# Hybrid S5 and gMLP encoder layer on one core: the setup transposes of b and c emitted by turns, each group at a tick of its own

## The chip, the core and the metric

The kernel runs on one core of a Trainium2 chip. The metric is the time of one execution in device microseconds (us). The engines of the core are named as the profile names them: PE (TensorE: matmuls, and transposes written as matmuls), PEld (its weight loads), DVE (VectorE), ACT (ScalarE), POOL (GpSimd) and SP (SyncE, which here only issues DMAs). Each engine runs its own list of instructions in order, and instructions of different engines wait for each other by semaphores.

## The reference

One encoder layer, batch 1, 512 positions, model width 1024, all in float32. An RMS norm of x goes through one wide projection w_in, whose columns feed two mixers and two gates. What the change touches is the S5 mixer:

```python
def s5_scan(u, lam_re, lam_im, log_step, b_re, b_im, c_re, c_im, reverse):
    lam = lax.complex(lam_re, lam_im)
    step = jnp.exp(log_step)[:, None]
    lam_bar = jnp.exp(lam * step)
    b_bar = ((lam_bar - 1.0) / lam)[..., None] * lax.complex(b_re, b_im)
    bu = jnp.einsum('gpc,lbgc->lbgp', b_bar, u.astype(jnp.complex64))
    _, states = lax.associative_scan(_linear_recurrence, (a, bu), axis=0, reverse=reverse)
    return jnp.einsum('gcp,lbgp->lbgc', lax.complex(c_re, c_im), states).real
...
    y = jax.nn.gelu(y.transpose(1, 0, 2, 3).reshape(bsz, seq, S5_WIDTH))
    y = y * jax.nn.sigmoid(y @ w_glu.astype(f32))
```

There y holds the D skip, the forward scan and the backward scan. There are 32 groups of 16 channels, each with 64 complex states, in two directions. The second mixer is a gMLP spatial gate (layer norm, a 128 x 128 mixing matrix for each head). The outputs of both are projected (w_proj_a, w_proj_b), gated per channel and added; after that come a cross-attention to 256 memory tokens and a SwiGLU feed-forward layer.

## The kernel before

**Matmuls.** Every large product of float32 operands is three products of rounded halves: an operand is split into hi and lo, hi by a copy on ScalarE (`split`, L85), lo by a subtraction on VectorE (L86). The products hi*hi, lo*hi and hi*lo are summed in PSUM (`mm3`, L358; `product`, L1110). Weights are loaded in blocks of 512 KB into `wraw` (L137, L224), split into `whi` and `wlo`, and used once. A plan lists all blocks in the order of use; `next_w` keeps three loads and two splits ahead of the block in use. PSUM has five banks for the main products and three for the others.

**Stages.** The stages are: norm of x and transposes of it into xn; the w_in products (pt and pf tiles); the w_proj_b products of the gMLP half, which are done with fewer and larger sums of blocks (tiles bx, bq and qv at L1110, with the operands s12 and s4 made by L85 and L86 and a `seed` copy into each qv bank at L1123); then the merge stage, where S5's output enters: four loads ygt (L1222) bring it back from DRAM, they are split into yg_hi and yg_lo, and the w_glu product (L358, pf<-yg_hi) gives the GLU. After that w_proj_a, the output projection, the attention and the feed-forward layer.

**The S5 side program.** S5 is not a stage of its own. `s5_program` is a Python generator: setup, kernels, inputs, scan and outputs yield between small pieces, and these pieces are put between the matmuls of the main stages. After each weight block the main program calls `tick(us)` (L453). A tick adds credit in proportion to the block's matmul time and then runs the generator until the credit is used up; a piece that yields a number costs that much credit, and one that yields None ends the side program's turn until the next tick. Further steps are put off by `later(n, ...)`, n ticks long. The pieces are:

- `s5_setup` (L620): loads of the steps and of lam, b and c; transposes of b and c through PSUM (tile pbc) with copies on ScalarE into raw_b and raw_c; then the powers of lam.
- `s5_kernels`: the tables e, pk, ks and tt of the 16-position blocks (L790 to L846).
- `s5_inputs`: wt by transposes (pw, L864), the products pz (L871), copies into zh (L876, L877).
- `s5_scan` (L893): 62 steps of four operations on VectorE (L898 to L901).
- `s5_outputs`: copies ss of the states (L916, L917), products py (L922 to L924), a gelu y (L929), and stores of y to the DRAM tile yd (L932), for four groups of eight.

`finish_side` runs what is left of it right before the merge stage.

**The order of the instructions.** The Python order is not yet the order on the engines: the framework's scheduler (`schedule_with_timeline_sim=True`) reorders the instructions by a timeline that it estimates, and keeps only those of `keep_in_program_order` as they are written. Among these are the late gain loads g_mem and g_x (`gain`, L471) and the first matmuls. So a step that is emitted some ticks later can change the order of everything that is scheduled after it, on every engine and in SP's list of DMAs.

Of the kernel before, what the change touches and what calls it, by code (L numbers as in the profile page):

```python
# [9 lines left out]
F32 = mybir.dt.float32  # L10
# [7 lines left out]
P = 128  # L18
# [8 lines left out]
G = 32  # L27
C = 16
# [24 lines left out]
def hybrid_layer_kernel(  # L53
# [8 lines left out]
    nc = tc.nc  # L62
# [14 lines left out]
    def bank(name):  # L77
        return pm.tile([P, 512], F32, tag="mm", name=name)

    def aux(name, shape=(P, 512)):  # L80
        return pa.tile(list(shape), F32, tag="aux", name=name)
# [394 lines left out]
    ident = cp.tile([P, P], F32, name="ident")  # L476
# [72 lines left out]
    s5p = s5.enter_context(tc.tile_pool(name="s5", bufs=1))  # L549
# [70 lines left out]
    def s5_setup():  # L620
        A_ = nc.scalar
# [3 lines left out]
        def small():  # L625
            used[0] += 1
            return slab[:, used[0] - 1, :]
# [6 lines left out]
        for i, src in enumerate((s5_lam_re, s5_lam_im)):  # L634
            nc.sync.dma_start(lrows[:, i], src[0].rearrange("d g p -> g d p"))
            ps = aux("plam", (P, G))
# [11 lines left out]
        crow = s5p.tile([P, 2, C // 4, 2, 64], F32, tag="tt", name="crow")  # L648
# [2 lines left out]
                nc.sync.dma_start(crow[:, i, :, d, :], src[0, d].rearrange("g (a b) p -> (g a) b p", a=4))  # L651
        bb = s5p.tile([P, 2, G, C], F32, name="raw_b")
        rows = brow.rearrange("g d p c -> g (d p) c")
        for n in range(2):
            ps = aux("pbc", (P, C // 2, 2 * G))
            for k in range(C // 2):
                nc.tensor.transpose(ps[:, k, :], rows[:, :, 8 * n + k], ident[:2 * G, :2 * G])
            A_.copy(bb.rearrange("p i g c -> p c (i g)")[:, 8 * n:8 * n + 8, :], ps)
            yield None
        cc = s5p.tile([P, 2, G, C], F32, name="raw_c")  # L660
        for i in range(2):
            ps = aux("pbc", (P, C // 4, P))
            for k in range(C // 4):
                nc.tensor.transpose(ps[:, k, :], crow[:, i, k].rearrange("q d p -> q (d p)"), ident)
            A_.copy(cc[:, i].rearrange("p g (a b) -> p b (g a)", a=4), ps)
            yield 0.1
        br, bi, cr, ci = bb[:, 0], bb[:, 1], cc[:, 0], cc[:, 1]
        st["c"] = (cr, ci)

# [1 line left out]
        stp, a, rho, th, n, sn, hs, cs = (small() for _ in range(8))  # L671
# [265 lines left out]
    def s5_program():  # L937
        yield from s5_setup()
        yield from s5_kernels(0)
        yield from s5_kernels(1)  # L940
        while "u" not in st:
            yield None
        zh = s5p.tile([P, NCH, 2, G], F32, name="zh")
        st["zh"] = zh
        for o in range(NO):
            yield from s5_inputs(o)
        while st.get("nz", 0) < 2 * NO:
            yield None
        yield None
        yield from s5_scan()  # L950
        for _ in range(2):
            yield None
        for o in range(NO):
            yield from s5_outputs(o)
            if o + 2 < NO:
                yield from s5_kernels(o + 2)
# [103 lines left out]
    for h in range(H):  # L1060
        ps = bank("psv")
# [56 lines left out]
    def unit_bank(name):  # L1118
        return bank(name).rearrange("p (j t) -> p j t", j=2)
# [45 lines left out]
    for q, ts in ((5, T1), (6, T0)):  # L1165
        for i in range(2):
            k = slice(2 * i, 2 * i + 2)
# [319 lines left out]
    for t0 in (0, 2):  # L1487
        ps = {t: bank(f"pt{t - t0}") for t in (t0, t0 + 1)}
# [77 lines left out]
    ps = [bank("pf0"), bank("pf1")]  # L1566
# [67 lines left out]
    for i, u in enumerate(UNITS):  # L1634
        final = i == len(UNITS) - 1
        x, v = begun
        q = unit_bank("pq")
# [132 lines left out]
    for i in range(2):  # L1770
        p = aux("pcut", (P, 256))
# [37 lines left out]
```

## Time and profile before

| what | value |
|---|---|
| median of 3 runs | 892.44 us (892.33 to 893.95) |
| profiled execution | 893.12 us, span 891.3 us, 1.8 us outside the span |
| granted clock, mean | 0.997 |
| PE busy | 881.1 us, 99% of the span |
| DVE busy | 642.5 us, 72% |
| ACT busy | 487.4 us, 55% |
| moved by DMA | 165.36 MB, mean 186 GB/s |
| scan on DVE | 154.10 to 244.53 us |
| first w_glu matmul | 326.10 us |

Times in the rows of the profile count from the start of the span. A row of the timeline has the start, the duration, the engine, the line of the kernel, the operation, the tiles (out<-in), the shapes and the count; in brackets stands how long the engine sat idle before it and what released it. A row of waits has the waiting engine, tile and line, what it waited for, the total, the count and the longest. A row of windows has, for PE, PEld, DVE, ACT and POOL in this order, the busy time and the count, then the granted clock of PE, the DMA share and GB/s. Successive matmuls overlap in the rows: the time that one costs is the distance from start to start, which is less than its duration. SPq is SP's DMA queue.

### The profile page before, as it was taken

How to read it: one execution, taken by the hardware profiler on the slowest of the kernel's cores; microseconds unless marked ns; L12 is line 12 of the kernel's file. 1: busy time of each engine (PE TensorE's matmuls, PEld its weight loads, DVE VectorE, ACT ScalarE, POOL GpSimd, SP SyncE). 2: the span in 40 equal slices, each digit the busy share in tenths (PEclk: the TensorE clock that was granted, in tenths of full speed). 3: DMA queues.
4: the chain of work that ended last, by engine and by line, in shares of the span. 5: the costliest groups of instructions: out<-in, count | busy, mean ns of one | idle time of the engine just before them, and what ended most of it. 6: DMA issues, size and time to landing. Idle time of an engine off the chain costs nothing.

```text
span 891.3 us, 14796 instructions
## 1 busy us (share of the span) xinstructions
PE 881.1 (99%) x5744; PEld 788.0 (88%) x5744; DVE 642.5 (72%) x1048; ACT 487.4 (55%) x714; POOL 106.9 (12%) x165
## 2 busy tenths in 40 slices
PE   9999999999999999999999999999999999999996
PEld 6788888888889998889899978999999999988875
DVE  5697653889847368658856836676878777899875
ACT  5743994244396254347656534645555455655664
POOL 1005301111032111001001001101121111000010
PEclk9999999999999999999999999999999999999998
DMA  8667456978533789834579747627899999356672
GB/s 255 196 189 182 114 155 177 189 191 190 159 87 84 212 285 268 288 117 140 168 221 256 194 103 197 166 81 181 213 237 233 216 225 249 95 167 207 204 230 102
DMA packets 118408, 165.36 MB, mean 186 GB/s; under 512 B 11825, under 2 KB 84161, under 8 KB 118210
## 3 DMA queue, kind: packets, MB, share of 16 engines
q1 hardware_dynamic: 97474, 135.74, 47.9%
q0 software_dynamic: 20576, 28.15, 19.9%
q8 instruction: 45, 0.74, 0.3%
q10 hardware_dynamic: 288, 0.52, 0.2%
q14 instruction: 25, 0.20, 0.1%
HBM read 157.61 MB, written 46.63 MB: 229 GB/s over the span
## 4 chain that ended last, share of the span: by engine, by line
PE 97%; DMA 1%; SPq 1%; ACT 0%; DVE 0%; issue 0%; POOLq 0%; ACTq 0%
PE pf L358 26%; PE pt L358 17%; PE px L1110 12%; PE dx L358 6%; PE pq L1110 6%; PE dq L358 3%; PE pv L1110 3%; PE bx L1110 3%; PE qx L1110 2%; PE dv L358 2%; PE pz L871 2%; PE pk L814 2%; PE bq L1110 1%; PE qv L1110 1%; PE psc L358 1%; PE qq L1110 1%
## 5 line engine op out<-in xcount | busy, mean ns | idle before, releaser
L86 DVE TENSOR_TENSOR wlo<-wraw,whi 128x1024 fp32r<-128x1024 f32 (+1 forms) x145 | 172.2, 1189 | 101.2 <-ACT whi L85 101.0
L85 ACT CAST whi<-wraw 128x1024 fp32r<-128x1024 f32 (+1 forms) x145 | 148.6, 1026 | 152.2 <-PE pf L358 44.0
L358 PE MATMUL pf<-xn,whi 128*128 128x512 f32 x448 | 139.6, 391 | 0.0
L358 PEld LDWEIGHTS pf<-xn,whi 128*128 128x128 f32 x448 | 83.7, 188 | 17.0
L358 PE MATMUL pf<-xn,wlo 128*128 128x512 f32 x224 | 87.3, 390 | 0.0
L1110 PE MATMUL px<-fn,whi 128*128 128x256 f32 x480 | 83.4, 277 | 0.0
L1110 PEld LDWEIGHTS px<-fn,whi 128*128 128x128 f32 x480 | 72.7, 188 | 0.2
L85 ACT CAST whi<-b 128x1024 fp32r<-128x1024 f32 x40 | 42.2, 1055 | 50.4 <-PE px L1110 27.4
L86 DVE TENSOR_TENSOR wlo<-b,whi 128x1024 fp32r<-128x1024 f32 x40 | 48.9, 1223 | 27.0 <-ACT whi L85 27.0
L1110 PE MATMUL px<-fn,wlo 128*128 128x256 f32 x240 | 66.4, 277 | 0.0
L1110 PE MATMUL pq<-s,whi 128*128 128x256 f32 x320 | 55.0, 276 | 0.0
L358 PE MATMUL dx<-whi,s 128*128 128x512 f32 x170 | 53.4, 390 | 0.4 <-DVE h L1734 0.4
L85 ACT CAST whi<-t 128x1024 fp32r<-128x1024 f32 x30 | 31.6, 1054 | 35.6 <-PE pv L1110 12.4
L86 DVE TENSOR_TENSOR wlo<-t,whi 128x1024 fp32r<-128x1024 f32 x30 | 36.7, 1225 | 19.7 <-ACT whi L85 19.7
L358 PEld LDWEIGHTS pf<-xn,wlo 128*128 128x128 f32 x224 | 42.1, 188 | 8.7
L1110 PEld LDWEIGHTS pq<-s,whi 128*128 128x128 f32 x320 | 48.3, 188 | 0.0
L1110 PEld LDWEIGHTS px<-fn,wlo 128*128 128x128 f32 x240 | 45.1, 188 | 0.0
L358 PE MATMUL pt<-whi,xn 128*128 128x512 f32 x128 | 43.7, 412 | 0.7 <-ACT xn L85 0.7
L1110 PE MATMUL pq<-s,wlo 128*128 128x256 f32 x160 | 44.2, 276 | 0.0
L358 PEld LDWEIGHTS dx<-whi,s 128*128 128x128 f32 x170 | 31.8, 188 | 7.5 <-issue 0.8
L358 PE MATMUL dx<-wlo,s 128*128 128x512 f32 x85 | 33.0, 390 | 0.0
L275 POOL DMA_DIRECT2D dsum<-in_w_down_dram x12 | 13.3, 1105 | 162.4 <-DMA dsum<-in_w_down_dram 162.4
(453 smaller groups left out, 2296.8 us busy)
## 6 DMA issues: line engine op xcount, KB each, us to landing
wraw<-in_w_in_dram SPq DMA_DIRECT2D x36, 512.0 KB, 4.7
dsum<-in_w_down_dram SPq DMA_DIRECT2D x20, 512.0 KB, 5.4
wraw<-dsum SPq DMA_DIRECT2D x20, 512.0 KB, 4.1
b<-in_w_gate_dram SPq DMA_DIRECT2D x15, 512.0 KB, 5.4
b<-in_w_up_dram SPq DMA_DIRECT2D x15, 512.0 KB, 5.3
wraw<-in_w_down_dram SPq DMA_DIRECT2D x15, 512.0 KB, 4.4
dsum<-in_w_down_dram POOLq DMA_DIRECT2D x10, 512.0 KB, 8.1
dsum<-dsum POOLq DMA_DIRECT2D x10, 512.0 KB, 8.5
```

Of the source, the lines that this page charges most:

```text
L85: hi = nc.scalar.copy(dst_hi, src)
L86: lo = nc.vector.tensor_tensor(dst_lo, src, dst_hi.bitcast(F32), ALU.subtract)
L275: plan[j + step][1].append((0, lambda d=dst, x=more: nc.gpsimd.dma_start(d, x, accum_op=ALU.add)))
L358: m = nc.tensor.matmul(ps, a[x], b[y], start=start and i == 0, stop=stop and i == 2, skip_group_check=free)
L814: nc.tensor.matmul(ps[32 * j:32 * j + 32, q, :], bd[i][:, g].rearrange("p d c -> p (d c)"), lc(es[i], g), start=(i == 0), stop=False, tile ...
L871: nc.tensor.matmul(ps[:, g, :], wt[:, g, :], u[:, o * GO + g, :], start=True, stop=True)
L1110: nc.tensor.matmul(ps[:, j, :], a[x], b[y], start=start and j == k == i == 0, stop=k == 3 and i == 2, skip_group_check=True)
```

## The change

In `s5_setup`, the transposes of b and c used to come as b, b, c, c, with a None after each b group and 0.1 us of credit after each c group. Now a None stands after the loads, ahead of the first transposes, and the groups come as b, c, b, c with a None after each. The transposes, copies and loads are the same, and the tile raw_c is allocated earlier.

```diff
         rows = brow.rearrange("g d p c -> g (d p) c")
+        cc = s5p.tile([P, 2, G, C], F32, name="raw_c")
+        yield None
         for n in range(2):
             ps = aux("pbc", (P, C // 2, 2 * G))
             for k in range(C // 2):
                 nc.tensor.transpose(ps[:, k, :], rows[:, :, 8 * n + k], ident[:2 * G, :2 * G])
             A_.copy(bb.rearrange("p i g c -> p c (i g)")[:, 8 * n:8 * n + 8, :], ps)
             yield None
-        cc = s5p.tile([P, 2, G, C], F32, name="raw_c")
-        for i in range(2):
             ps = aux("pbc", (P, C // 4, P))
             for k in range(C // 4):
-                nc.tensor.transpose(ps[:, k, :], crow[:, i, k].rearrange("q d p -> q (d p)"), ident)
-            A_.copy(cc[:, i].rearrange("p g (a b) -> p b (g a)", a=4), ps)
-            yield 0.1
+                nc.tensor.transpose(ps[:, k, :], crow[:, n, k].rearrange("q d p -> q (d p)"), ident)
+            A_.copy(cc[:, n].rearrange("p g (a b) -> p b (g a)", a=4), ps)
+            yield None
         br, bi, cr, ci = bb[:, 0], bb[:, 1], cc[:, 0], cc[:, 1]
```

## The prediction

> **What bounds the kernel now.** I read the page first (span, busy shares, the chain that ended last), then TensorE's waits.
>
> ```profile
> span 891.3 us, 14796 instructions
> PE 881.1 (99%) x5744; PEld 788.0 (88%) x5744; DVE 642.5 (72%) x1048; ACT 487.4 (55%) x714; POOL 106.9 (12%) x165
> ...
> PE 97%; DMA 1%; SPq 1%; ACT 0%; DVE 0%; issue 0%; POOLq 0%; ACTq 0%
> ```
>
> ```profile
> PE idle L556 <- DVE mhalf L481: 1.1, 1, 1.1
> PE pt L358 <- ACT ot_hi L85: 0.9, 2, 0.7
> PE pt L358 <- ACT xn L85: 0.7, 1, 0.7
> PE dx L358 <- DVE h L1734: 0.4, 1, 0.4
> ```
>
> TensorE is busy 99% of the span, it carries 97% of the chain, and its waits come to 1.1 + 0.9 + 0.7 + 0.4 = 3.1 us in all. The kernel is TensorE's list of matmuls with nothing between them. The first wait stands ahead of all code in question. So a change of order can win at most about 2 us here, and it loses whatever hole it opens in that list. The question is only: which instruction of TensorE finds its operand late in the new order?
>
> **The transposes themselves.** The change keeps all of them: 16 of b and 8 of c, and four copies out of PSUM on ScalarE.
>
> ```profile
> 30.93 1.09 PE L657 MATMUL pbc<-ident,brow 64*128 64x64 f32 x8
> ...
> 35.99 0.60 PE L664 MATMUL pbc<-ident,crow 128*128 128x128 f32 x4
> ```
>
> Per group they take 1.09 and 0.60 us, before and after: nothing added, nothing removed, 0 us in the sum. What the edit changes is when the S5 side program gets past them. A bare yield ends the side program's turn until the next tick. There were two such yields (after the b groups) and two that cost 0.1 us of credit; now there are five, the new first one ahead of any transpose. So the rest of the S5 chain (parameters, powers, input products, scan) is emitted about three ticks later, and the planner builds another order out of it on all engines. Comparing the two orders of instructions, engine by engine, I find the following.
>
> **The scan starts 6.6 us later.** The scan on VectorE waits for the last pz products and their copies.
>
> ```profile
> 149.99 1.89 PE L871 MATMUL pz<-u,wt 128*128 128x64 f32 x16
> ```
>
> ```profile
> 154.10 0.22 DVE L898 TENSOR_TENSOR sa<-zh,ca 128x64 f32<-128x64 f32 x1 [2.16 <-ACT zh L877]
> ...
> 244.30 0.23 DVE L901 TENSOR_TENSOR zh<-sa,sb 128x64 f32<-128x64 f32 x1
> ```
>
> Ahead of the last pz, TensorE's list now holds 29 more pf matmuls of 512 columns (272 where there were 243). A matmul of that size takes 0.23 us from start to start: in the rows below two of them lie between 13.19 and 13.65.
>
> ```profile
> 11.51 0.63 PE L358 MATMUL pt<-wlo,xn 128*128 128x512 f32 x1
> 11.94 0.98 PE L358 MATMUL pt<-whi,xn 128*128 128x512 f32 x2
> ...
> 13.19 0.62 PE L358 MATMUL pt<-whi,xn 128*128 128x512 f32 x2
> 13.65 0.40 PE L358 MATMUL pt<-wlo,xn 128*128 128x512 f32 x1
> ```
>
> 29 x 0.227 = 6.6 us. The scan's own length does not change (244.53 - 154.10 = 90.4 us), so it ends at about 244.5 + 6.6 = 251.1. TensorE had other work throughout the scan before, and its list is full there after too; this delay alone costs nothing. It matters by what stands behind it.
>
> **First hole: qv after the scan.** The first qv product of the merged w_proj_b part started at 277.11. Behind the scan, ScalarE's rows before are:
>
> ```profile
> 244.56 1.10 ACT L916 COPY ss<-zh 64x504 f32<-64x504 f32 x1 [0.88 <-DVE zh L901]
> ...
> 253.37 1.05 ACT L85 CAST whi<-wraw 128x1024 fp32r<-128x1024 f32 x1
> ...
> 255.87 1.28 ACT L929 ACT_TABLE_LOAD   x1
> 257.16 0.60 ACT L929 ACTIVATE y<-py 128x512 f32<-128x512 f32 x1
> 257.65 1.11 ACT L916 COPY ss<-zh 64x504 f32<-64x504 f32 x1
> ...
> 264.11 2.18 ACT L85 CAST s<-zf 128x512 fp32r<-128x512 f32 x4
> ...
> 268.57 0.58 ACT L1123 COPY qv<-bx 128x512 f32<-128x512 f32 x1
> ```
>
> ```profile
> 255.25 0.39 PE L923 MATMUL py<-ss,e 128*128 128x64 f32 x2
> ...
> 255.92 0.39 PE L923 MATMUL py<-ss,e 128*128 128x64 f32 x2
> ...
> 265.52 0.49 PE L814 MATMUL pk<-e,bd 128*32 128x128 f32 x3
> ...
> 265.99 0.49 PE L814 MATMUL pk<-e,bd 128*32 128x128 f32 x3
> ...
> 277.11 0.28 PE L1110 MATMUL qv<-yb_hi,whi 128*128 128x256 f32 x1
> ...
> 278.05 0.28 PE L1110 MATMUL qv<-yb_hi,wlo 128*128 128x256 f32 x1
> ```
>
> Before, the copy that fills the qv bank was done at 269.15, 8 us ahead of its use. After, TensorE gets there earlier: 24 py matmuls and 15 pairs of pk pieces that stood ahead now stand behind. Three py take 255.92 - 255.25 = 0.67, so 24 are 5.3 us; two pairs of pk take 0.47, so 15 are 3.5 us. Demand: 277.1 - 5.3 - 3.5 = 268.3. ScalarE's list from the scan's end to that copy is now: eight ss copies (244.56 to 253.37, 8.8), part 0.5 (as y, which is as large), four s copies 2.2, part 0.5, one whi 1.0, table load 1.3, y 0.5, four more ss copies 4.5, two s copies 1.1, one whi 1.0, qv 0.6: 22.0 us, so it is ready at 273.1. TensorE waits 273.1 - 268.3 = 4.8, with one pk piece in the middle, whose e operand VectorE rebuilds late. A weight cast that now stands at the scan's end may hold the chain up by 1 us more. I take 5.0; bounds 0 (if the scan starts as before, or ScalarE gets ahead) and 7.
>
> **Second hole: the next qv.** After the second group of py, ScalarE's order is four ss copies, a whi cast, the copy for qv; the copies are released by the last py, as in
>
> ```profile
> 275.25 1.13 ACT L916 COPY ss<-zh 64x504 f32<-64x504 f32 x1 [1.33 <-PE py L924]
> ```
>
> 4 x 1.13 + 1.05 + 0.58 = 6.2 us. TensorE has 34 matmuls of 256 columns and one pk to run meanwhile; eight take 278.05 - 277.11 = 0.94, so 34 are 4.0, and 4.2 with the pk. It waits 2.0 us; bounds 0 and 3.
>
> **Third and largest hole: the GLU's input.** The last S5 outputs go through DRAM (yd) and come back as four ygt loads; a cast of each feeds the first GLU matmul.
>
> ```profile
> 318.44 1.77 SPq L1222 DMA_DIRECT2D ygt<-yd  x4
> ...
> 331.33 0.53 SPq L471 DMA_DIRECT2D g_x<-in_xattn_norm_g_dram  x1
> ```
>
> ```profile
> 330.19 0.68 DVE L1173 TENSOR_TENSOR part<-zf,part 128x512 f32<-128x512 f32 x1
> ```
>
> ```profile
> 326.10 0.63 PE L358 MATMUL pf<-yg_hi,whi 128*128 128x512 f32 x2
> ```
>
> ```profile
> 330.00:336.00 6.00, 6.00 (x28) 4.99 (x27) 3.35 (x5) 3.37 (x6) 1.20 (x1) 1.00 1.06 385
> ```
>
> ```profile
> wraw<-in_w_proj_a_dram SPq DMA_DIRECT2D x4, 512.0 KB, 8.4
> ...
> ygt<-yd SPq DMA_DIRECT2D x4, 256.0 KB, 4.1
> ...
> yd<-y SPq DMA_DIRECT2D x4, 32.0 KB, 2.3
> ```
>
> Before, the ygt loads were issued at 318.44, behind only the two w_glu loads, 7.7 us ahead of the GLU at 326.10, which then did not wait. In the new order of SP's queue they stand behind w_proj_a, qsum, w_proj_a, g_mem and g_x. g_x waits for the L1173 that closes the part tile, as the rows show (330.19 + 0.68, then 331.33), and that L1173 waits for the last bq matmul, the one directly ahead of the GLU on TensorE. So the ygt loads can only be issued after TensorE has run dry. Call that moment G. Two operations of 0.68 (L1132, L1173) with their starts end at G + 1.6; g_x takes 0.53; the first ygt is issued at G + 2.2. Best landing: the 4.1 us of before, then a cast of 0.55: G + 6.9. Worst landing: the 8.4 us that loads took in the crowd: G + 11.2. For the middle I count bytes: five loads of 512 KB, the first two from about G - 3; at 385 GB/s some 1.4 MB are through by G + 2.2, 1.2 MB and the first 0.26 MB remain, 3.8 us, or up to 6.1 us with the 2.3 us that even a small yd store needs. With the cast: G + 6.6 to G + 8.9. I take 7.8; bounds 6 and 11. The three other ygt land 0.7 us apart and the next stage's operands are made behind the late GLU: another 0.8, bounds 0 and 2.
>
> **The clock.** At the end of the span the granted clock falls after TensorE has stopped:
>
> ```profile
> 884.20:884.70 0.50, 0.24 (x3) 0.04 (x1) 0.24 (x2) 0.23 (x2) 0.50 (x1) 1.00 0.00 0
> ...
> 886.50:886.80 0.30, 0.00 (x0) 0.00 (x0) 0.00 (x0) 0.00 (x0) 0.30 (x1) 0.50 0.00 0
> ```
>
> The last matmul ends at 884.44 (0.24 us into the first row); 2 us later the clock is 0.50. And at the start the matmuls of the first dense 3 us run at half the rate (11.51 to 11.94: 0.43 for one) until about 12.7. So the first and the third hole, both longer than 2 us, should each be followed by about 3 us at half rate, in which 1.5 us of work is lost: 3.0 us for two; bounds 0 and 4.
>
> [...]
>
> **Sum.** 5.0 + 2.0 + 7.8 + 0.8 + 3.0 = 18.6 us on the profiled execution's 893.1 (span 891.3 and 1.8 around it): 911.7. The median of the runs shown is 0.7 lower, so I predict 911.
>
> **Rivals.**
> (a) Only the GLU hole opens. If ScalarE reaches the qv copies 5 us sooner than I count, or the scan loses less than 2 us, the first two holes close: 7.8 + 0.8 + 1.5 = 10.1, about 902.5. For it: the first hole is a difference of two long sums. Against it: the scan's shift is a plain count of matmuls.
> (b) All holes open and the ygt loads meet the full crowd: hole 11, tail 2, the clock lower for 4 us after each: 5 + 2 + 11 + 2 + 4 = 24, about 916.5. For it: 1.06 of DMA share around 330. Against it: the crowd before consisted of loads that are now behind ygt.
> (c) No difference: every late operand is covered. That needs the ygt loads issued at least 7 us ahead of G, against their place behind g_x. 892.4.
> (d) Faster: the later S5 chain lets ScalarE deliver the xn and ot_hi casts in time, and no hole opens. The two waits are 1.6 us together, so 890.8. It decides only if the ygt loads are issued before G - 7, and the two waits lie in stages whose order hardly changes.
>
> **Chances.** The forecast with its own range 907 to 915: 0.55; (a) 0.22; (b) 0.14; (c) 0.03; (d) 0.06. A difference below 0.2% (1.8 us) can't be told from none here. Faster 0.06, same 0.03, slower 0.91. The range takes in (a) and (b) and 1.5 us below and above them, for the bounds of their own holes: 901 to 918.
>
> **What would show it.** Right: in TensorE's waits a pf L358 <- yg_hi (or ygt) line of 6 to 11 us, and qv L1110 <- ACT qv L1123 lines of 3 to 7 us together; ygt issued after g_x, later than the last bq matmul; last L901 near 251; half clock in the windows after the holes; after 345 us everything shifted by the same 18 us. Wrong: ygt ahead of g_x, the last L901 at 245, or 0.2 us matmuls directly behind a hole of 8 us (then 3 us less).

## The result, and the profile after

The changed kernel takes 917.3 us (median of five runs, 915.4 to 919.4) against 892.7 (892.3 to 894.0): ratio 1.0273, 95% interval 1.0255 to 1.0291, so 24.6 us slower. The forecast was 911, range 901 to 918. The profiled execution is the slowest of the five: 919.42, span 917.7, 26.4 us over the span before.

The page of the changed kernel (span, busy shares), and TensorE's waits:

```profile
span 917.7 us, 14794 instructions
...
PE 887.4 (97%) x5744; PEld 792.5 (86%) x5744; DVE 643.6 (70%) x1048; ACT 485.2 (53%) x712; POOL 106.8 (12%) x165
```

```profile
PE pf L358 <- ACT yg_hi L85: 9.4, 1, 9.4
PE pk L814 <- DVE e L795: 4.4, 1, 4.4
PE qv L1110 <- ACT qv L1123: 3.3, 2, 1.8
PE pt L358 <- ACT xn L85: 2.3, 1, 2.3
```

The three holes are there, at the three tiles named: 9.4 us ahead of the GLU, 4.4 for one pk piece and 1.5 more for the first qv, 1.8 for the second qv; 17.1 us in all, where the kernel before had none of them. The timeline shows the GLU hole's cause in the rows of VectorE, SP's queue, ScalarE and TensorE:

```profile
341.15 0.69 DVE L1173 TENSOR_TENSOR part<-zf,part 128x512 f32<-128x512 f32 x1
```

```profile
341.87 0.35 SPq L471 DMA_DIRECT2D g_x<-in_xattn_norm_g_dram  x1
342.64 1.96 SPq L1222 DMA_DIRECT2D ygt<-yd  x4
```

```profile
349.14 0.62 ACT L85 CAST yg_hi<-ygt 128x512 fp32r<-128x512 f32 x1 [7.79 <-DMA ygt<-yd]
```

```profile
340.11 0.28 PE L1110 MATMUL bq<-s,wlo 128*128 128x256 f32 x1
349.81 0.79 PE L358 MATMUL pf<-yg_hi,whi 128*128 128x512 f32 x1 [9.43 <-ACT yg_hi L85]
```

TensorE's last bq matmul ends at 340.39; only then can the last L1173 run (by way of L1132, which reads bq), behind it g_x, and behind that, 2.25 us after TensorE went dry, the first ygt load. Its cast starts 6.5 us after that issue and takes 0.6: together the 9.4 us of the hole.

Most of what is left of the loss is the clock. In windows (PE, PEld, DVE, ACT, POOL busy with counts, then the granted clock, DMA share, GB/s):

```profile
277.40:281.40 4.00, 3.95 (x18) 3.95 (x19) 3.04 (x3) 0.97 (x1) 0.00 (x0) 0.50 0.40 131
281.50:285.50 4.00, 4.00 (x37) 4.00 (x37) 3.13 (x4) 1.36 (x2) 0.00 (x0) 1.00 0.40 130
...
302.00:305.30 3.30, 3.30 (x16) 3.30 (x17) 3.30 (x4) 1.76 (x3) 2.10 (x4) 0.50 0.50 70
...
343.00:349.80 6.80, 0.00 (x0) 0.00 (x0) 0.01 (x1) 0.62 (x1) 1.34 (x2) 0.50 1.02 311
349.80:353.10 3.30, 3.29 (x8) 2.61 (x9) 1.87 (x3) 1.24 (x2) 0.00 (x0) 0.50 1.14 279
353.20:357.00 3.80, 3.80 (x18) 3.11 (x18) 0.79 (x2) 1.90 (x2) 0.00 (x0) 1.00 1.09 392
```

Behind each hole, the second one too, matmuls ran at half clock: 18 of them instead of 37 in four us behind the first. The stretches of work at half clock are 4.0, 3.4 and 3.3 us, so 2.0 + 1.7 + 1.7 = 5.4 us were lost there.

One part of the profiled run does not come from the change. In its first 24 us the order is that of before, but a row that stood at 18.19 before (`pt<-whi,xn`, three matmuls) stands at

```profile
18.86 0.80 PE L358 MATMUL pt<-whi,xn 128*128 128x512 f32 x1 [2.31 <-ACT xn L85]
...
21.59 1.07 PE L358 MATMUL pt<-whi,xn 128*128 128x512 f32 x3
```

3.4 us later, behind a wait of 2.31 us for xn (ScalarE sat 1.74 us behind a late load of the S5 steps) and a stretch at half clock, from 18.64 to 22.05. Other kernels below have the same order there and start without it, or have it with no edit there.

The account of the profiled run: start 3.4, holes 17.1, half clock 5.4, waits inside and behind the GLU 1.0 (its stage, from the start of the first yg_hi matmul to the start of the last ya matmul, took 32.46 us before and 35.10 after; 1.7 of the 2.64 us more are the clock): 26.9 against a span that grew by 26.4.

### The profile page after: what moved, and what is told of

It is laid out like the page before. It is cut to its first block, busy times and chain, and to the rows that moved or that the text cites. A ratio compares the mean times of both kernels' runs of the same rounds, so it can differ in the third digit from the quotient of the medians.

```text
span 917.7 us, 14794 instructions
## 1 busy us (share of the span) xinstructions
PE 887.4 (97%) x5744; PEld 792.5 (86%) x5744; DVE 643.6 (70%) x1048; ACT 485.2 (53%) x712; POOL 106.8 (12%) x165
## 4 chain that ended last, share of the span: by engine, by line
PE 67%; ACT 1%; DMA 1%; issue 1%; DVE 1%; SPq 0%; POOLq 0%; ACTq 0%; DVEq 0%
PE pt L358 12%; PE px L1110 12%; PE pf L358 9%; PE dx L358 6%; PE pq L1110 6%; PE dq L358 3%; PE pv L1110 3%; PE qx L1110 2%; PE bx L1110 2%; PE dv L358 2%; PE qv L1110 2%; PE psc L358 1%; PE qq L1110 1%; PE po L358 1%; PE ptr L520 1%; PE bq L1110 1%
## 5 line engine op out<-in xcount | busy, mean ns | idle before, releaser
L358 PEld LDWEIGHTS pt<-whi,xn 128*128 128x128 f32 x128 | 24.9, 197 | 9.4 <-ACT xn L85 2.9
```

The source lines that it names most:

```text
L358: m = nc.tensor.matmul(ps, a[x], b[y], start=start and i == 0, stop=stop and i == 2, skip_group_check=free)
```

## Experiments

**1. Which part of the edit costs: the tick or the turns?** One kernel takes only the new yield, in the order b, b, c, c; one takes only the turns, with the old number of ticks.

```diff
-        rows = brow.rearrange("g d p c -> g (d p) c")
+        rows = brow.rearrange("g d p c -> g (d p) c"); yield None
         for n in range(2):
```

> The kernel before (groups b, b, c, c with their old yields) with one edit: the bare yield ahead of the first transposes. Theory (what costs is that the S5 side program falls a tick behind; the turns of b and c cost nothing): the same holes as in the changed kernel, TensorE waits of 9 to 10 us at the GLU for yg_hi, 5 to 6.5 us for the pk and the first qv, 1.5 to 2 us at the second qv, last L901 about 10 us later than in the kernel before in a run whose start is equal 6 us, and a time of 915 to 920. Rival (the emission by turns costs, through the order of the copies on ScalarE): 892 to 894, no such wait.

Measured: 916.9 us (916.1 to 917.0; ratio 1.0254, 1.0225 to 1.0283). TensorE's waits:

```profile
PE pf L358 <- ACT yg_hi L85: 9.2, 1, 9.2
PE pk L814 <- DVE e L795: 4.4, 1, 4.4
PE qv L1110 <- ACT qv L1123: 3.3, 2, 1.8
```

The bare yield alone gives all holes to 0.2 us. Its profiled run has no late start: span 915.3, scan from 160.64 to 250.77, its start 6.5 us later than before.

The turns alone are the changed kernel with these lines put back:

```diff
         cc = s5p.tile([P, 2, G, C], F32, name="raw_c")
-        yield None
...
             A_.copy(cc[:, n].rearrange("p g (a b) -> p b (g a)", a=4), ps)
-            yield None
+            yield 0.1
```

> The changed kernel without its bare yield ahead of the first transposes and with the old 0.1 after each c group: b, c, b, c by turns, but as many ticks as before. Theory (the ticks): 892 to 894, scan starts at 154, ygt loads ahead of g_x, no wait at the GLU. Rival (the turns): 910 or more, with the holes of the changed kernel.

Measured: 893.95 us against 894.42 for the kernel before on the same chip, ratio 0.9998 (0.9983 to 1.0013). No difference. The scan starts at 154.37, and SP's queue has the order of before from start to end:

```profile
318.59 1.77 SPq L1222 DMA_DIRECT2D ygt<-yd  x4
...
327.41 0.51 SPq L471 DMA_DIRECT2D g_mem<-in_mem_norm_g_dram  x1
...
331.47 0.53 SPq L471 DMA_DIRECT2D g_x<-in_xattn_norm_g_dram  x1
```

So emitting b and c by turns costs nothing, and the tick costs everything.

**2. Does it grow with the ticks?** Two more kernels add ticks in other places: one only replaces 0.1 by None after the c groups of the kernel before, the other has None after each of four groups by turns, without the first one.

```diff
-            yield 0.1
+            yield None
         br, bi, cr, ci = bb[:, 0], bb[:, 1], cc[:, 0], cc[:, 1]
```

> The kernel before with one edit: a bare yield after each c group instead of 0.1 of credit; order b, b, c, c. Theory (any tick more in the setup moves the scan behind the same later pz): the holes of the changed kernel, 915 to 918. Rival (only the tick ahead of the first transposes matters, since it delays the b copies): 892 to 896.

Measured: 918.9 us (a single run), waits for yg_hi 9.1, pk 4.4, qv 3.3. Its first 24 us hold the same late start as the changed kernel's profile (a 2.3 us wait for xn).

```diff
         cc = s5p.tile([P, 2, G, C], F32, name="raw_c")
-        yield None
         for n in range(2):
```

> The changed kernel without the yield ahead of the first transposes, but with a bare yield after each of the four groups. Theory (any tick more in the setup moves the scan by the same step): the holes of the changed kernel, 915 to 918. Rival (the loss grows with the number of ticks): less than the changed kernel, 900 to 912.

Measured: 917.9 us (a single run), waits 9.2, 4.4, 3.3. The kernel before and the turns alone have two bare yields; one has three, two have four, the changed kernel five. All beyond two show the same holes. The loss is a step, not a slope, and the b copies are not needed for it. The traces show why a step: from 172 us on (the scan has begun by then) the lists of instructions of all five engines are the same, place by place, in the four kernels with more than two bare yields. The planner comes to one and the same order from any of them; why it does was not tried.

**3. The GLU hole alone.** In the kernel before, g_mem and g_x are emitted ahead of the ygt loads, and those are kept behind them on SP. The S5 chain is as early as before.

```diff
+    g_mem, g_x = gain(mem_norm_g, "g_mem", True), gain(xattn_norm_g[0], "g_x", True)
     for m in range(4):
-        nc.sync.dma_start(ygt[:, m, :], yd[m].rearrange("p l n -> p (l n)"))
+        in_order(nc.sync.dma_start(ygt[:, m, :], yd[m].rearrange("p l n -> p (l n)")))
```

> The kernel before with g_mem and g_x emitted ahead of the four ygt loads, and these kept in that order on SP: the GLU hole alone, with the S5 chain as early as before. Theory: a wait for yg_hi of 9 to 11 us, half clock for 5 to 10 us around it, and nothing else: 903 to 906. Rival (the early S5 chain leaves slack that hides the loads' place): 892 to 896.

Measured: 908.2 us (907.3 to 909.0) against 894.4, ratio 1.0158 (1.0129 to 1.0187). The only new wait:

```profile
PE pf L358 <- ACT yg_hi L85: 11.7, 1, 11.7
```

The scan ends at 244.66 as before, the GLU starts at 338.04 instead of 326.10, and the clock is at half from 330.71 to 340.95, 2.9 us of it over work. The place of four loads in a queue, alone, costs 14 us; the span grew by 14.6: 11.7 of hole, 1.5 of clock, and 1.4 of which 1.1 lie behind the last ya matmul and were not followed up. The 906 I gave as the upper end is 2.2 us too low: the hole is longer than the 11 allowed, and longer than in the changed kernel. The first ygt load is issued 1.9 us after the last bq matmul here, so no later than there, but it takes 8.8 us to land (328.26 to 337.04).

**4. What holds the ygt loads in the changed kernel?** Here g_mem and g_x are queued behind the last ygt load.

```diff
-        nc.sync.dma_start(ygt[:, m, :], yd[m].rearrange("p l n -> p (l n)"))
+        ld = nc.sync.dma_start(ygt[:, m, :], yd[m].rearrange("p l n -> p (l n)"))
...
-    g_mem, g_x = gain(mem_norm_g, "g_mem", True), gain(xattn_norm_g[0], "g_x", True)
+    with tc.issue_after(ld.ins): g_mem, g_x = gain(mem_norm_g, "g_mem", True), gain(xattn_norm_g[0], "g_x", True)
```

> The changed kernel with g_mem and g_x queued on SP behind the last ygt load; the rest of the order stays. Theory (the GLU hole is made by the place of the ygt loads behind g_x, which waits for the last bq products): the ygt loads are issued about 2.5 us sooner against the last bq matmul, the hole falls from 9.4 to about 7, the time by 2 to 3 us, to 914 to 916. What is left of the hole then belongs to the later yd stores and the loads of w_proj_a and qsum ahead. Rival (g_x is not what holds them, the DMA traffic is): hole and time unchanged, 9 to 10 us and 916 to 919.

Measured: 912.7 us (911.5 to 913.1), ratio 1.0207 (1.0178 to 1.0236). The waits, and SP's rows:

```profile
PE pf L358 <- ACT yg_hi L85: 6.9, 1, 6.9
PE pk L814 <- DVE e L795: 4.4, 1, 4.4
PE qv L1110 <- ACT qv L1123: 3.3, 2, 1.9
```

```profile
335.36 3.19 SPq L1222 DMA_DIRECT2D ygt<-yd  x4
338.59 0.43 SPq L471 DMA_DIRECT2D g_mem<-in_mem_norm_g_dram  x1
339.12 0.37 SPq L471 DMA_DIRECT2D g_x<-in_xattn_norm_g_dram  x1
```

The first ygt load goes out 0.3 us after the last bq matmul (which ends at 335.04) instead of 2.25 us, and the hole falls by 2.5 us. 6.9 us remain without g_x. The w_proj_a and qsum loads stay ahead, and the last y is stored closer to the GLU: in the changed kernel its stores are issued from 334.56, 5.8 us ahead of G, where before it was 312.19, 13.9 us ahead of 326.10. How these two share the rest was not taken apart.

The time fell by 4.6 us between the medians, more than the 2 to 3 expected. The profile has no half clock behind the second hole, which this edit does not touch; by the account above that is worth 1.7 us (the last section shows where that hole lay in time).

**5. The holes behind the scan.** First, pins of order, meant to put the third group's ss copies behind the qv copy on ScalarE, and the s12 subtractions behind the rebuilding of e on VectorE. Pinned are one of the group's four copies and the casts and subtractions of s12.

```diff
-            nc.scalar.copy(s[lo_, :, 1:NCH], zv[lo_, :, 0:NCH - 1])
+            (in_order if o == 2 and i == 0 else (lambda q: q))(nc.scalar.copy(s[lo_, :, 1:NCH], zv[lo_, :, 0:NCH - 1]))
...
-            split(bops[q][0][:, k], bops[q][1][:, k], zf[i][:, :, ts])
+            pinned[0] = True; split(bops[q][0][:, k], bops[q][1][:, k], zf[i][:, :, ts]); pinned[0] = False
```

> The changed kernel with two pins of order after the scan: the third group's ss copies on ScalarE behind the qv copy, and the s12 subtractions on VectorE behind the rebuilding of e; the scan ends as late. Theory (the first hole is made by what stands ahead of the qv copy and of e in these two lists, 4.5 us of ss copies among it): no wait of pk for e, the first qv wait 3.5 to 5 us instead of 4.4 + 1.5, the second below 1.5, and 913 to 915.5. Rival (the late end of the scan alone makes the hole, whatever stands behind it): both waits as in the changed kernel, 916 to 918.

Measured: 915.0 us (913.4 to 915.4), ratio 1.0241 (1.0216 to 1.0265).

```profile
PE pf L358 <- ACT yg_hi L85: 9.6, 1, 9.6
PE qv L1110 <- ACT qv L1123: 5.7, 2, 4.4
```

The waits are as expected, but the pins did less than was meant. ScalarE's rows:

```profile
266.68 1.07 ACT L917 COPY ss<-zh 64x504 f32<-64x504 f32 x1
...
270.86 0.58 ACT L1123 COPY qv<-bx 128x512 f32<-128x512 f32 x1
...
273.36 1.10 ACT L916 COPY ss<-zh 64x504 f32<-64x504 f32 x1
```

Only the pinned copy, and two casts of s, now stand behind the qv copy; the group's other three copies are still ahead of it. On VectorE e comes no sooner: it is ready 21.0 us behind the scan's end, against 20.6 in the changed kernel. The wait for e is gone because the pk pair that waited stands behind the first qv products in TensorE's new list (at 276.78). So this run does not show that the order on VectorE made the wait. What moved is the qv copy: it is done 20.7 us behind the scan's end instead of 22.7, and the two qv waits are 4.4 and 1.3 us instead of 4.4 + 1.5 and 1.8. That is 2.0 us less, with the scan ending just as late. The time's interval overlaps that of the changed kernel; it is the rows that carry this.

Second, half of the ss copies go to GpSimd.

```diff
-            nc.scalar.copy(s[hi_, :, 0:NCH - 1], zv[hi_, :, 0:NCH - 1][:, :, ::-1])
+            nc.gpsimd.tensor_copy(s[hi_, :, 0:NCH - 1], zv[hi_, :, 0:NCH - 1][:, :, ::-1])
```

> The changed kernel with one of each two ss copies (L917) on GpSimd instead of ScalarE: ScalarE's list between the end of the scan and the qv copies is 4 to 6 copies of 1.1 us shorter. Theory (ScalarE's list makes the holes after the scan): pk and the second qv do not wait any more, the first qv waits 0 to 3 us, GLU hole as before at 9 to 11 us, 909 to 913. Rival (GpSimd is much slower at such a copy than ScalarE, so py comes late instead): new waits of py for ss, 915 or more.

Measured: 914.2 us (911.9 to 914.7), ratio 1.0231 (1.0208 to 1.0253); the expected 909 to 913 was missed. TensorE's waits:

```profile
PE pf L358 <- ACT yg_hi L85: 14.1, 1, 14.1
PE qv L1110 <- ACT qv L1123: 2.0, 1, 2.0
```

GpSimd does such a copy in 1.0 to 2.1 us, and no wait of py for ss appears. The holes behind the scan shrink from 7.7 to 2.0 us. ScalarE's list is confirmed as what made the qv waits: TensorE's last bq matmul ahead of the first hole ends 16.2 to 16.3 us behind the scan's end in the changed kernel, with the pins and here alike, while the first qv copy is done after 22.7, 20.7 and 18.2 us, and the hole follows it (e is sooner here as well, 16.3 us behind the scan: VectorE rebuilds it behind subtractions that sit idle for ScalarE's s casts, 8.7 us in the changed kernel; and the pk pair stands behind the first qv products again).

But 4.7 of these 5.7 us come back at the GLU, whose hole is now 14.1. TensorE gets there 7.3 us sooner than with the bare yield alone (the last bq matmul ends at 329.36 against 336.68), the first yg_hi matmul starts only 2.4 us sooner (343.50 against 345.86). That is not the sooner arrival alone, since SP has a new order too:

```profile
330.84 0.34 SPq L471 DMA_DIRECT2D g_x<-in_xattn_norm_g_dram  x1
331.98 0.38 SPq L137 DMA_DIRECT2D wraw<-in_w_proj_a_dram  x1
332.41 0.66 SPq L274 DMA_DIRECT2D qsum<-qsum  x1
333.49 2.69 SPq L1222 DMA_DIRECT2D ygt<-yd  x4
```

Two 512 KB loads now stand between g_x and ygt. The first ygt load goes out 4.1 us after the last bq matmul instead of 2.25, and lands 9.2 us later. How much would have come back with SP's old order is not shown. Together with the queue of experiment 4 (the edit is that diff and this one):

> Both remedies on the changed kernel: one of each two ss copies on GpSimd, and g_mem and g_x queued behind the ygt loads. Theory (holes and their queues explain the whole loss): the post-scan holes 0 to 3 us, the GLU hole 3 to 6 us, one or no stretch of half clock, 901 to 906. Rival (part of the loss is spread in small waits that these remedies do not touch): 909 or more.

Measured: 907.0 us (905.5 to 910.6), ratio 1.0161 (1.0132 to 1.0190).

```profile
PE pf L358 <- ACT yg_hi L85: 7.6, 1, 7.6
PE qv L1110 <- ACT qv L1123: 2.0, 1, 2.0
```

Between the medians both remedies take off 10 us; the GLU hole is larger than the 3 to 6 I expected, and with it the time by 1 us. 9.6 us of holes are left for a span 13.5 us over that of before; its profile has two stretches of half clock, from 269.56 and from 334.42, where I expected one or none. These kernels are remedies for a loss; none comes near the kernel before.

**6. The clock.** 34 unread matmuls of 512 columns stand in the GLU hole, between the last bq matmul and the first GLU matmul.

```diff
+    for _ in range(34): in_order(nc.tensor.matmul(aux("idle"), yb_hi[:, 0, 0:P], yb_hi[:, 4, :], start=True, stop=True))
     for c0 in range(0, SW, 256):
         feat(w_glu, c0, (yg_hi, yg_lo), 4, glu_evac)
```

> The changed kernel with 34 matmuls of 512 columns that nobody reads, placed on TensorE between the last bq matmul and the first GLU matmul, in the hole. Theory (the hole also lowers the granted clock, and the GLU then runs some 3.4 us at half rate): the matmuls fill 7.7 us of the 9.3, the wait for yg_hi reads 1.5 to 2 us, the clock stays at 1.00 around the GLU, the first GLU matmuls come 0.23 us apart instead of 0.43, and the time falls by 1.5 to 2 us against 917, to 915 to 916. Rival (the clock costs nothing beside the hole, since the next operands are late anyway): the same 917 as the changed kernel within 0.5 us.

Measured: 917.0 us (914.3 to 918.6), ratio 1.0264 (1.0238 to 1.0291), not the 915 to 916 expected. A gap of 2.47 us remained, and half clock followed it, as the windows show:

```profile
342.10:344.50 2.40, 0.00 (x1) 0.00 (x0) 0.00 (x0) 0.60 (x2) 0.00 (x0) 1.00 1.08 353
...
345.10:348.40 3.30, 3.30 (x9) 2.55 (x8) 2.13 (x4) 2.21 (x3) 0.00 (x0) 0.50 1.14 279
```

Behind the GLU's first products TensorE also waits 1.3 us for ya_hi here, a wait that the changed kernel does not have. With 44 of them (the same line with `range(44)`):

> As the kernel with 34 unread matmuls in the GLU hole, with 44 of them: 10.0 us, the whole hole. With 34 a gap of 2.5 us was left and the clock still fell, from 345.07 to 348.48. Theory (the fall of the clock behind the hole costs 1.7 us): no fall near the GLU, the stretch from the first to the last matmul on yg_hi is 10.7 us as in the kernel before instead of 12.3, and the time 1 to 1.7 us below 917. Rival (what follows the GLU is late anyway, so the clock's loss is hidden): the wait for ya_hi grows by as much as the GLU gains and the time stays at 917.

Measured: 917.4 us (914.8 to 921.3), ratio 1.0257 (1.0233 to 1.0281).

```profile
337.00:347.00 10.00, 8.82 (x41) 7.01 (x39) 2.52 (x3) 1.45 (x2) 1.34 (x2) 1.00 1.01 336
347.20:353.00 5.80, 5.72 (x25) 4.68 (x26) 2.68 (x4) 3.08 (x5) 0.00 (x0) 1.00 1.12 312
353.00:360.00 7.00, 7.00 (x32) 5.74 (x31) 2.41 (x3) 2.88 (x5) 1.17 (x1) 1.00 0.45 170
```

Now the clock stays full, and nothing is gained; but two things blur the comparison. Seven of the 44 were scheduled among the GLU's own matmuls (1.6 us), so from the first to the last yg matmul it took 12.5 us, as at half clock (12.3). And in both kernels the loads landed later: the first yg_hi matmul starts 10.2 us after the last bq matmul with 34 and 9.9 with 44, against 9.4 in the changed kernel and 9.2 with the bare yield alone. Behind the GLU hole, the clock's 1.7 us are thus not shown to be a loss beside the late loads. The rival is not shown either: the wait for ya_hi did not grow with 44 (there is none), perhaps because the seven matmuls fill the time. Whether TensorE at full rate would have waited for the later casts of yg_hi, which start 0.5 to 1.5 us apart (346.61 to 349.56), is open. Behind the first hole the operands were ready, and there the windows show the loss directly.

## Why the prediction was right, and which terms were off

- **"Nothing added by the transposes, all by the tick"**: shown by the pair of experiment 1.
- **The scan 6.6 us later**: 6.5 in the profile of the bare yield alone; 10.2 in the changed kernel's own, with 3.4 of its start in it.
- **First hole, 5.0**: 5.84. ScalarE's chain from the scan's end to the qv copy was counted as 22.0 us and took 22.66 (254.74 to 277.40), with the weight cast at the scan's end that I allowed up to 1 us for: it held the ss copies back by 0.9. TensorE wanted the bank 16.2 us behind the scan's end, where the prediction has 268.3 - 251.1 = 17.2: the demand came 1 us sooner than counted. The order in which pk comes first was right: 4.4 of the 5.8 are its wait for e.
- **Second hole, 2.0**: 1.8.
- **GLU hole, 7.8**: 9.4. The issue at G + 2.2 was right to 0.05 us, and so was the cast (0.62 us against 0.55). The landing was short: 7.8 - 2.2 - 0.55 leaves 5.05 us from the first issue to its cast, and it took 6.5 (342.64 to 349.14). I had counted the 512 KB loads ahead at 385 GB/s; during the hole the windows show 311. The upper end of the count by bytes, 6.1 us, was nearer than the middle that I took; the 8.4 us of the crowd came true only for the later three loads (7.3 to 9.4 us) and in experiments 3 and 5 (8.8 and 9.2 us for the first).
- **The clock, 3.0**: the mis-sized term. I charged two falls with 1.5 us each; there were three, and the work at half clock sums to 10.7 us, so 5.4, above the bound of 4. The step "holes longer than 2 us" failed at the second hole: half clock followed one of 1.84 us. How much of the last 1.7 would have been waited for anyway is open (experiment 6).
- **Rest, 0.8**: 1.0.

Together the named terms give 18.6 by the prediction and 23.5 as measured, against 24.6 in the medians. The forecast's own range (907 to 915) was missed by 2.3 us, by the landing and the clock. The result lies in the wide range by 0.7 us, in the room that was left for rival (b); so the mechanism was right, and that the number fits is in part luck. Rival (b) names 916.5, near the result, but by a GLU hole of 11 and a tail of 2, which did not come; its 4 us for the clock were nearer to the 5.4 than the 3.0. Rival (a), closed holes behind the scan, was not the case, and in experiment 5, where they were nearly closed, most of their time came back at the GLU, with another order on SP as well. The faster and the unchanged case needed the ygt loads ahead of G - 7; they were issued at G + 2.25.

## What to carry to other kernels

In a kernel whose bound engine never waits, an edit that only moves side work by a tick is judged by the places where that work's late end meets a queue in order: list what stands ahead of each of its consumers, above all DMAs issued behind one that waits for the bound engine itself (their place alone cost 14 us in experiment 3). Here the holes cost their length, 17.1 us, and up to 5.4 us more at half clock behind them; and of 5.7 us of holes that were closed early in the program, 4.7 came back at the next meeting point, with another order on SP as well (experiment 5). Where only a schedule moved, separate the parts of the edit first: here a single bare yield carried all of it.

## What the hardware showed that was not expected

- **Half clock behind short holes.** Holes of 1.8 to 1.9 us at the second qv were followed by half clock in five of seven profiles with such a hole, and not in two (experiments 4 and 6, the latter with 34 matmuls). The clock records tell them apart. In the changed kernel the changes of the clock from the first hole on come at 274.64, 281.46, 301.94, 305.36, 342.90 and 353.14 us: 78.50 us that divide into 23 steps of 3.413, with 2, 6, 1, 11 and 3 of them between one change and the next. Counted in such steps from each profile's own changes, in the five the whole hole lies inside one step, in which TensorE is idle for 1.84 to 1.86 us. In the two, the end of a step cuts the hole, into 1.29 and 0.56 us (experiment 4) and 1.66 and 0.18 us (experiment 6). The step with the hole and the next one, first with the bare yield alone, then in experiment 4:

```profile
295.07:298.48 3.41, 1.56 (x12) 1.17 (x12) 1.12 (x2) 3.37 (x5) 0.00 (x0) 1.00 0.35 82
298.49:301.89 3.40, 3.40 (x18) 3.40 (x17) 3.40 (x5) 1.55 (x3) 2.10 (x4) 0.50 0.54 75
```

```profile
294.15:297.56 3.41, 2.12 (x18) 1.73 (x17) 1.18 (x2) 3.36 (x5) 0.00 (x0) 1.00 0.41 93
297.57:300.97 3.40, 2.84 (x24) 2.84 (x25) 3.35 (x3) 2.45 (x5) 2.08 (x4) 1.00 0.36 54
```

  In the profiles of the kernel before and of the changed one, from 30 us on, half clock followed each step at full clock that held more than 0.9 us of idle TensorE: one of 2.04 us at the end of the span before, and 3.41, 1.84, 2.51 and, at the end of the span, 2.11 us in the changed kernel. Four steps at the ends of other spans, with 1.74 to 1.86 us, were not followed by it. In the first 30 us even steps with 1.24, 1.42 and 1.50 us were (the turns alone, the first kernel of experiment 2, experiment 4), and these steps hold the four early matmuls whose operands have one row. No run moved a hole against these steps on purpose, so this is what went together in these profiles, and a cause is not shown.
- **Start of a run.** With the same order of instructions, the first 24 us differed by 3.4 us between profiles, through one late small load (ScalarE sat 1.74 us behind it in the changed kernel's profile) and a stretch at half clock (18.64 to 22.05).
- **GpSimd copies** of 64 x 504 elements took 1.0 to 2.1 us, with four in a row 5.2 us, beside 1.1 us for one on ScalarE.
